# Row operations of the norms on VectorE instead of GpSimd, and two attention heads weighed side by side

## The chip, the cores and the metric

The kernel runs on one core of a Trainium2 chip. The metric is the device time of one execution in microseconds (us), as the median of several runs. A core has five engines that run in parallel and meet by semaphores: TensorE (PE in the profile, with its weight loads as PEld), VectorE (DVE), ScalarE (ACT), GpSimd (POOL) and SyncE (SP), whose queue here issues the DMAs.

## The reference, cut to what matters

Two layers work on 256 latent tokens (a grid of 4 rows of 64) and 256 context tokens, all of width 1024 in float32.

- Layer 0 mixes the tokens with 8 heads of neighbourhood attention (head width 64) beside 4 heads of a bidirectional recurrence (HGRN2), then a dense SwiGLU feed-forward layer (FFN).
- Layer 1 mixes with 4 heads of retention, then a top-2-of-8 SwiGLU mixture of experts.

```python
# neighbourhood attention: one softmax over the grid window and all context keys
p = softmax(concat([q @ k_band + bias, q @ k_ctx]))        # latent queries: 512 keys
o = p[band] @ v_band + p[ctx] @ v_ctx
a_c = full_attention(nc_q, nc_k, nc_v)                      # context queries: 256 keys
# after each of the four sub-layers (post-norm)
x = layer_norm(ALPHA * x + gate * y) * g + b
ctx = layer_norm(ALPHA * ctx + gate_c * y_c) * g + b        # layer 0 only
```

## The kernel before

All weights come from HBM by DMAs on SP's queue. Most float32 products are made of three matmuls on "fp32r" operands (`mm3`, lines 128 to 130): a value is split into a rounded high part (ScalarE copies it, `whi`) and a rest (VectorE subtracts, `wlo`). Such a matmul has one TensorE instruction; a plain float32 matmul has two. The order of instructions on each engine is set at build time by a list scheduler that may interleave stages; each engine then runs its list strictly in order.

The stages, with their times in the profile:

- **Layer 0 mixing (to about 362 us).** For each of 4 indices, `head_in` projects one HGRN head and runs its chain, and `pair(j)` projects and runs two attention heads (`na_pair`, line 569). For head `i` of a pair the tile `qs[:, i]` holds the high part of the queries in 64 partitions and their rest in the other 64, and `ks[:, i]` holds the high part of the keys in both halves. `score` (lines 581 to 584) makes one matmul over 128 partitions (high and rest of q times high of k) and one over 64 partitions (high of q times the rest of k, `kl`). Scores of 128 latent queries get their bias (L594), a softmax (`softmax`, L557 to L566), four transposes (L598), a copy to SBUF (L599), and are weighed with the values in `pm` (L603), one head after the other: each head writes 64 of the 128 output columns of the array, at `tile_position=(0, 64 * i)`. The context queries follow (L611 to L615). `ax_new` hands out the two PSUM banks of scores and transposes.
- **Output projection, norm, FFN (362 to 800 us).** `after0(i)` normalises row tile `i` of the residual stream `R` (tiles 0 and 1 latent, 2 and 3 context, 128 x 1024 each). `spread` transposes tiles into `h` for the next layer (ScalarE writes the high part, VectorE the rest, L236). The norm's scale and shift reach `h` by other coefficients, so that `R` itself needs `g` and `b` only at its next addition. That is `finish_ln`: two GpSimd operations for each row tile (L666, L667). For the latent tiles it is called right behind their `spread`, for the context tiles in `spread_ctx0`, and again in `after1` behind the FFN.
- **Retention (800 to about 1085 us)**, by heads `hd`, with weights through a ring of four buffers `raw` (`wload`).
- **Routing and experts (from about 1085 us).** `rows_in` (line 1118) writes the normalised rows in a high part and a rest (`xnl`, a GpSimd subtraction, L1125). `residual` (line 1060) scales and shifts `R` on GpSimd during the first expert.

```python
def finish_ln(i):
    nc.gpsimd.tensor_mul(R[i], R[i], lnrow[0])
    nc.gpsimd.tensor_add(R[i], R[i], lnrow[1])
```

Of the kernel before, what the change touches and what calls it, by code (L numbers as in the profile page):

```python
# [16 lines left out]
D = 1024  # L17
KD = 8
T = 512
# [69 lines left out]
def hybrid_kernel(ctx: ExitStack, tc: tile.TileContext, a, out):  # L89
# [479 lines left out]
    def na_pair(j, pq, pk, pt_new, pm):  # L569

        qs, ks = (phg.tile([128, 2, T], F32R, name=nm, tag=nm) for nm in ("qs", "ks"))
        kl = phg.tile([128, T], F32R, name="kl", tag="kk")
        for i in range(2):
            r, z = slice(64 * i, 64 * i + 64), slice(64 - 64 * i, 128 - 64 * i)
            nc.scalar.mul(qs[r, i, :], pq[r, :], 0.125)
            nc.vector.scalar_tensor_tensor(qs[z, i, :], pq[r, :], 0.125, qs[r, i, :], op0=OP.mult, op1=OP.subtract)
            nc.scalar.copy(ks[r, i, :], pk[r, :])
            nc.scalar.copy(ks[z, i, :], pk[r, :])
            nc.vector.tensor_sub(kl[r, :], pk[r, :], ks[r, i, :])

        def score(S, i, qc, kc):
            r = slice(64 * i, 64 * i + 64)
            nc.tensor.matmul(S, qs[:, i, qc], ks[:, i, kc], start=True, stop=False)
            nc.tensor.matmul(S, qs[r, i, qc], kl[r, kc], start=False, stop=True)

        for i in range(2):
            hh = 2 * j + i
            bias = arr("bias", [128, 2, 256])
            nc.sync.dma_start(bias, a["bias"][hh].rearrange("(t p) k -> p t k", p=128))
            pt2 = arr("pt2", [128, 4, 256])  # L590
            for t in range(2):
                S = ax_new()
                score(S, i, slice(t * 128, t * 128 + 128), slice(0, T))
                nc.vector.tensor_add(S[:, 0:256], S[:, 0:256], bias[:, t, :])  # L594
# [4 lines left out]
                nc.scalar.copy(pt2[:, :, t * 128:t * 128 + 128], pt.rearrange("p (c q) -> p c q", c=4))  # L599
            r = slice(64 * i, 64 * i + 64)  # L600
            vs = slice(hh * 64, hh * 64 + 64)
            for c in range(4):
                nc.tensor.matmul(pm[r, 0:256], nv[:, c, vs], pt2[:, c, :], start=(c == 0), stop=(c == 3), tile_position=(0, 64 * i))  # L603
            S = ax_new()
            for t in range(2):
                score(S[:, t * 256:t * 256 + 256], i, slice(256 + t * 128, 256 + t * 128 + 128), slice(256, T))
            E = softmax(S, 2, 256)
            pt = pt_new()
            for t in range(2):
                for c in range(2):  # L610
                    nc.tensor.transpose(pt[:, c * 256 + t * 128:c * 256 + t * 128 + 128], E[:, t * 256 + c * 128:t * 256 + c * 128 + 128], ident)  # L611
            ptc = phg.tile([128, 2, 256], F32, name="ptc", tag="f0")
            nc.scalar.copy(ptc, pt.rearrange("p (c q) -> p c q", c=2))
            for c in range(2):
                nc.tensor.matmul(pm[r, 256:512], nv[:, 2 + c, vs], ptc[:, c, :], start=(c == 0), stop=(c == 1), tile_position=(0, 64 * i))  # L615
        put_mix(j, pm)
# [47 lines left out]

    def finish_ln(i):
        nc.gpsimd.tensor_mul(R[i], R[i], lnrow[0])  # L666
        nc.gpsimd.tensor_add(R[i], R[i], lnrow[1])  # L667

# [6 lines left out]
    def after0(i):  # L675
        normalise(pb, R[i], "ln0")
        if i == 2:
            spread(0, "f0", h)
            finish_ln(0)
            finish_ln(1)  # L680

# [5 lines left out]
    def spread_ctx0():  # L687
        spread(1, "f0", h)
        finish_ln(2)
        finish_ln(3)  # L690

# [24 lines left out]
    for half, (t0, t1) in enumerate(((0, 6), (6, 11))):  # L716
# [3 lines left out]
        for f in range(nf):  # L720
# [11 lines left out]
            else:  # L732
                ada_next(0 if j < 8 else 1)
                for x, w in zip(p, wt):
                    mul_T(x, w, h, slice(0, 512))
            u = pb.tile([128, T], F32, name="u", tag="u", bufs=2)
            nc.scalar.activation(u, p[0], AF.Silu)
# [3 lines left out]
        if half:  # L741
# [12 lines left out]
            h = new_h("h1", KD, T)  # L754
            ln_rows(0, 1)

        def after1(i):
            normalise(pb, R[i], "ln1")
            if i == 2:
                spread(0, "a1", h)  # L760
                finish_ln(0)
                finish_ln(1)

# [8 lines left out]
    def spread_ctx1():  # L772
        spread(1, "a1", h)


# [58 lines left out]
    for hd in range(4):  # L834
# [56 lines left out]
        if hd:  # L891
            gates(hd)
        og = cnew("og", [128, 2, 512], 1)
        for t in range(2):
# [165 lines left out]
    def residual():  # L1060
# [551 lines left out]
```

## Time and profile before

| | |
|---|---|
| median of 3 runs | 2005.65 us (2003.67 to 2009.47) |
| the profiled execution | 2005.2 us, its span 2003.4 us |
| mean granted TensorE clock | 0.980 of full speed |
| busy, share of the span | PE 96%, PEld 69%, DVE 62%, ACT 41%, POOL 4% |
| DMA | 510 MB, mean 255 GB/s |

The span is the time from the first to the last instruction of the profiled execution; 1.8 us lie around it. A busy PE is not a PE at its peak: an instruction counts from its start to its modelled end, and successive matmuls overlap, so the pace of matmuls is read from one start to the next. "<-" behind an idle time names what ended it.

### The profile page before, as it was taken

How to read it: one execution, taken by the hardware profiler on the slowest of the kernel's cores; microseconds unless marked ns; L12 is line 12 of the kernel's file. 1: busy time of each engine (PE TensorE's matmuls, PEld its weight loads, DVE VectorE, ACT ScalarE, POOL GpSimd, SP SyncE). 2: the span in 40 equal slices, each digit the busy share in tenths (PEclk: the TensorE clock that was granted, in tenths of full speed). 3: DMA queues.
4: the chain of work that ended last, by engine and by line, in shares of the span. 5: the costliest groups of instructions: out<-in, count | busy, mean ns of one | idle time of the engine just before them, and what ended most of it. 6: DMA issues, size and time to landing. Idle time of an engine off the chain costs nothing. (4 is left out here: it accounts for less than half of the span.)

```text
span 2003.4 us, 24686 instructions
## 1 busy us (share of the span) xinstructions
PE 1926.9 (96%) x9143; PEld 1374.8 (69%) x9143; DVE 1241.9 (62%) x2020; ACT 830.8 (41%) x1080; POOL 78.6 (4%) x71
## 2 busy tenths in 40 slices
PE   8999999979999999899999999999999999999995
PEld 4887776658878878788888437853588338878731
DVE  4747775684587667865656518850588138888703
ACT  3435554233332332634433216730476026777500
POOL 0010000120000000100000210000000010000000
PEclk9999999989999999899999899999899999999998
DMA  7322233653356553323358899999999999999896
GB/s 296 137 92 88 91 98 107 215 199 128 124 167 208 185 185 116 127 85 116 111 201 310 324 414 396 375 345 420 418 416 367 388 420 420 413 341 375 316 410 241
DMA packets 94896, 510.00 MB, mean 255 GB/s; under 512 B 11312, under 2 KB 14000, under 8 KB 51760
## 3 DMA queue, kind: packets, MB, share of 16 engines
q1 hardware_dynamic: 94768, 508.34, 67.5%
q8 instruction: 74, 1.21, 0.3%
q14 instruction: 54, 0.44, 0.1%
HBM read 507.25 MB, written 1.05 MB: 254 GB/s over the span
## 5 line engine op out<-in xcount | busy, mean ns | idle before, releaser
L974 DVE TENSOR_TENSOR mlo<-mraw,mhi 128x2048 fp32r<-128x2048 f32 x168 | 378.3, 2286 | 37.5 <-ACT mhi L970 37.3
L202 ACT CAST whi<-raw 128x1024 fp32r<-128x1024 f32 x170 | 178.4, 1052 | 363.7 <-PE bank L129 216.0
L970 ACT CAST mhi<-mraw 128x2048 fp32r<-128x2048 f32 x168 | 312.3, 1910 | 24.0 <-PE bank L130 24.0
L203 DVE TENSOR_TENSOR wlo<-raw,whi 128x1024 fp32r<-128x1024 f32 x170 | 208.5, 1229 | 122.4 <-ACT whi L202 119.2
L130 PE MATMUL bank<-h0h,wlo 128*128 128x512 f32 (+1 forms) x656 | 250.7, 383 | 9.4 <-DVE wlo L203 9.4
L128 PE MATMUL bank<-h0h,whi 128*128 128x512 f32 (+1 forms) x656 | 252.1, 385 | 4.8 <-ACT whi L202 4.6
L129 PE MATMUL bank<-h0l,whi 128*128 128x512 f32 (+1 forms) x656 | 251.1, 383 | 4.5 <-DVE h0l L236 4.5
L1260 DVE TENSOR_TENSOR g<-g,bank 64x512 f32<-64x512 f32 x28 | 19.0, 679 | 236.6 <-ACT g L1259 236.6
L1256 PE MATMUL bank<-mraw,xg_145.75_15_12_8059 128*64 128x512 f32 x672 | 154.5, 601 | 0.8 <-DMA mraw<-in_moe_w 0.8
L130 PEld LDWEIGHTS bank<-h0h,wlo 128*128 128x128 f32 x656 | 126.5, 193 | 32.1 <-DVE wlo L203 10.2
L128 PEld LDWEIGHTS bank<-h0h,whi 128*128 128x128 f32 x656 | 125.6, 192 | 31.0 <-ACT whi L202 5.2
L129 PEld LDWEIGHTS bank<-h0l,whi 128*128 128x128 f32 x656 | 126.0, 192 | 28.2 <-DVE h0l L236 5.5
L128 PE MATMUL bank<-mhi,xg_145.75_15_14_8404 128*128 128x512 f32 x336 | 134.0, 400 | 4.9 <-ACT mhi L970 4.9
L129 PE MATMUL bank<-mlo,xg_145.75_15_14_8404 128*128 128x512 f32 x336 | 135.5, 403 | 2.5 <-DVE mlo L974 2.4
L128 PE MATMUL bank<-whi,h0h 128*128 128x512 f32 x288 | 114.7, 401 | 2.2 <-ACT whi L202 1.6
L130 PE MATMUL bank<-whi,h0l 128*128 128x512 f32 x288 | 113.9, 396 | 0.0
L129 PE MATMUL bank<-wlo,h0h 128*128 128x512 f32 x288 | 113.2, 395 | 0.0
L1256 PEld LDWEIGHTS bank<-mraw,xg_145.75_15_12_8059 128*64 128x64 f32 x672 | 47.4, 138 | 92.1 <-issue 88.7
L1259 ACT ACTIVATE g<-bank 64x512 f32<-64x512 f32 x28 | 16.6, 594 | 222.2 <-PE bank L1256 222.2
L130 PE MATMUL bank<-mhi,xg_145.75_15_15_8405 128*128 128x512 f32 x224 | 89.2, 398 | 0.0
L130 PE MATMUL bank<-mhi,xg_145.75_15_16_9605 128*128 128x512 f32 x224 | 88.6, 396 | 0.0
L129 PEld LDWEIGHTS bank<-mlo,xg_145.75_15_14_8404 128*128 128x128 f32 x336 | 64.8, 193 | 20.6 <-DVE mlo L974 5.9
(518 smaller groups left out, 3378.8 us busy)
## 6 DMA issues: line engine op xcount, KB each, us to landing
mraw<-in_moe_w SPq DMA_DIRECT2D x336, 1024.0 KB, 8.5
aw<-in_ada_u SPq DMA_DIRECT2D x96, 512.0 KB, 4.4
raw<-in_o_w_nat SPq DMA_DIRECT2D x32, 512.0 KB, 3.6
raw<-in_ffn_w1T SPq DMA_DIRECT2D x22, 512.0 KB, 4.6
raw<-in_ffn_w3T SPq DMA_DIRECT2D x22, 512.0 KB, 3.6
raw<-in_ffn_w SPq DMA_DIRECT2D x22, 512.0 KB, 3.7
raw<-in_e_w_T SPq DMA_DIRECT2D x20, 512.0 KB, 3.6
raw<-in_o_w_T SPq DMA_DIRECT2D x16, 512.0 KB, 3.6
```

What stands on the lines that cost most here:

```text
L128: nc.tensor.matmul(ps, l[0], r[0], start=first, stop=False)
L129: nc.tensor.matmul(ps, l[0], r[1], start=False, stop=False)
L130: return nc.tensor.matmul(ps, l[1], r[0], start=False, stop=last)
L202: nc.scalar.copy(hi, raw)
L203: nc.vector.tensor_sub(lo, raw, hi)
L970: x = nc.scalar.copy(hi, raw)
L974: y = eng.tensor_sub(lo[:, c], raw[:, c], hi[:, c])
L1256: nc.tensor.matmul(ps[64 * m:64 * m + 64, :], x[:, kk, :], w[:, k, :], start=(kk == 0), stop=(kk == KD - 1), tile_position=(0, 64 * m))
L1259: silu.append(nc.scalar.activation(g, ps[64:128, :], AF.Silu))
L1260: nc.vector.tensor_mul(g, g, ps[0:64, :])
```

## The change

- `finish_ln` becomes eight half-width operations for two row tiles on VectorE (four for each tile, 128 x 512 each). For the four tiles of layer 0's first norm it is called in the FFN's blocks 2 to 5, one tile in each. For the two latent tiles of the second norm it is called in the retention's head 1 (`rows_ready`), from two rows loaded into two of the four `raw` buffers; the load into `lnrow` is dropped. `residual` uses it too, and `rows_in` subtracts on VectorE.
- In `na_pair` the loop over query tiles goes outside, the loop over heads inside. `kl` is one tile for each head, its rest of k in both halves, so that the second matmul of `score` also takes 128 partitions (that adds the product of the two rests). The weighing of both heads is issued together, alternating between the two halves of the array's columns (`weigh`): for each 128 latent queries, and once for the 256 context queries. The bias is loaded for both heads and one query tile at a time, the same bytes.

```diff
     def finish_ln(i, rows):
-        nc.gpsimd.tensor_mul(R[i], R[i], lnrow[0])
-        nc.gpsimd.tensor_add(R[i], R[i], lnrow[1])
+        for c in (slice(0, 512), slice(512, D)):
+            nc.vector.tensor_mul(R[i][:, c], R[i][:, c], rows[0][:, c])
+            nc.vector.tensor_add(R[i][:, c], R[i][:, c], rows[1][:, c])
...
# after0, spread_ctx0, after1
-            finish_ln(...)
# FFN, block j
+                if 2 <= j < 6:
+                    finish_ln(j - 2, lnrow)
# before after1
-            ln_rows(0, 1)
+    def rows_ready():
+        rows = [wp.tile([128, D], F32, name="raw", tag="raw", bufs=4) for _ in range(2)]
+        for t, nm in zip(rows, ("ln_g", "ln_b")):
+            nc.sync.dma_start(t, a[nm][0, 1:2, :].to_broadcast([128, D]))
+        for i in range(2):
+            finish_ln(i, rows)
# retention, behind gates(hd)
+        if hd == 1:
+            rows_ready()
# residual
-            nc.gpsimd.tensor_mul(R[i], R[i], t[:, 0, :])
-            nc.gpsimd.tensor_add(R[i], R[i], t[:, 1, :])
+            finish_ln(i, (t[:, 0, :], t[:, 1, :]))
# rows_in
-            nc.gpsimd.tensor_sub(xnl[:, i, c], R[i][:, c], xnh[:, i, c])
+            nc.vector.tensor_sub(xnl[:, i, c], R[i][:, c], xnh[:, i, c])
# na_pair
-            nc.vector.tensor_sub(kl[r, :], pk[r, :], ks[r, i, :])
+            for x in (r, z):
+                nc.vector.tensor_sub(kl[i][x, :], pk[r, :], ks[r, i, :])
...
-            nc.tensor.matmul(S, qs[r, i, qc], kl[r, kc], start=False, stop=True)
+            nc.tensor.matmul(S, qs[:, i, qc], kl[i][:, kc], start=False, stop=True)
...
+        def weigh(c, first, last, cols, p):
+            for i in range(2):
+                vs = slice((2 * j + i) * 64, (2 * j + i) * 64 + 64)
+                nc.tensor.matmul(pm[64 * i:64 * i + 64, cols], nv[:, c, vs], p[i], start=first, stop=last, tile_position=(0, 64 * i))
+        for t in range(2):
+            q = slice(t * 128, t * 128 + 128)
+            nc.sync.dma_start(bias, a["bias"][2 * j:2 * j + 2, q].rearrange("h p k -> p h k"))
+            for i in range(2):
...                                  # score, bias, softmax, transposes, copy of head i
             for c in range(4):
-                nc.tensor.matmul(pm[r, 0:256], nv[:, c, vs], pt2[:, c, :], start=(c == 0), stop=(c == 3), tile_position=(0, 64 * i))
+                weigh(c, c == 0, c == 3, q, [pt2[:, i, c, :] for i in range(2)])
...                                  # both heads' context scores, then
+        for c in range(2):
+            weigh(2 + c, c == 0, c == 1, slice(256, 512), [x[:, c, :] for x in ptc])
```

The new tiles share addresses with tiles of the HGRN head: the second `kl` with its `f1`, the second `ptc` with its `q` (the first ones already shared with `kk` and `f0`).

## Rows read from the trace of the kernel before

**Rows 1.** Windows: length, busy PE, PEld, DVE, ACT, POOL; clock, DMA share, GB/s.
```profile
134.00:362.00 228.00, 227.19 (x1215) 162.90 (x1216) 157.70 (x410) 111.89 (x203) 0.00 (x0) 1.00 0.31 101
398.60:440.40 41.80, 28.18 (x196) 21.71 (x196) 34.30 (x63) 17.46 (x30) 15.29 (x7) 0.84 0.51 172
803.70:820.00 16.30, 9.43 (x53) 8.86 (x52) 14.06 (x30) 9.50 (x13) 4.38 (x2) 0.69 0.22 66
480.00:600.00 120.00, 120.00 (x538) 95.89 (x537) 77.12 (x148) 39.16 (x92) 0.00 (x0) 1.00 0.42 137
850.00:1040.00 190.00, 190.00 (x955) 161.09 (x954) 109.54 (x211) 80.33 (x108) 10.61 (x8) 1.00 0.37 117
1130.00:1200.00 70.00, 69.13 (x332) 25.22 (x328) 24.84 (x82) 12.32 (x29) 12.98 (x12) 1.00 1.01 413
```
**Rows 2.** Timeline of PE, a score of 512 keys: start, length, line, shapes.
```profile
177.98 0.39 PE L130 MATMUL bank<-h0h,wlo 128*128 128x512 f32 x1
178.21 0.39 PE L583 MATMUL bank<-ks,qs 128*128 128x512 f32 x1
178.52 0.50 PE L584 MATMUL bank<-kl,qs 64*128 64x512 f32 x1
178.95 0.38 PE L532 MATMUL bank<-hv,attc 128*128 128x128 f32 x1
```
**Rows 3.** Timeline of PE, scores of context queries, 256 keys.
```profile
181.23 0.38 PE L583 MATMUL bank<-ks,qs 128*128 128x256 f32 x1
181.55 0.38 PE L584 MATMUL bank<-kl,qs 64*128 64x256 f32 x1
181.86 0.38 PE L583 MATMUL bank<-ks,qs 128*128 128x256 f32 x1
```
**Rows 4.** Timeline of PE, the weighing of one head, latent then context queries.
```profile
184.26 1.94 PE L603 MATMUL bank<-pt,nv 128*64 128x256 f32 x8
186.13 0.66 PE L611 MATMUL bank<-ident,E 128*128 128x128 f32 x4
...
189.65 1.08 PE L615 MATMUL bank<-ptc,nv 128*64 128x256 f32 x4
```
**Rows 5.** Timeline of PE and PEld in the small expert: matmuls in both column halves.
```profile
1162.75 0.60 PE L1256 MATMUL bank<-mraw,xg_145.75_15_12_8059 128*64 128x512 f32 x2
1163.18 3.60 PE L1245 MATMUL bank<-mraw,_145.75_178.75_16_4_8147 128*64 128x512 f32 x16
...
1163.18 0.14 PEld L1245 LDWEIGHTS bank<-mraw,_145.75_178.75_16_4_8147 128*64 128x64 f32 x2 [0.28 <-issue]
```
**Rows 6.** Timeline of POOL and DVE behind the first norm.
```profile
394.14 4.95 POOL L666 TENSOR_TENSOR s_183.75_199.75_8_2_2622<-s_183.75_199.75_8_2_2622,nrow_183.75_9_0_2623 128x1024 f32<-128x1024 f32 x2 [286.25 <-ACT h0h L230]
...
396.82 2.56 DVE L236 TENSOR_TENSOR h0l<-tm_183.75_9_17_2995,h0h 128x256 fp32r<-128x256 f32 x1
...
404.51 0.42 DVE L236 TENSOR_TENSOR h0l<-tm_183.75_9_18_2999,h0h 128x256 fp32r<-128x256 f32 x1
```
**Rows 7.** Timeline of PE behind the first norm, its two longest waits.
```profile
407.18 0.58 PE L130 MATMUL bank<-h0h,wlo 128*128 128x256 f32 x1 [7.16 <-DVE wlo L203]
...
428.61 0.58 PE L129 MATMUL bank<-h0l,whi 128*128 128x256 f32 x1 [3.78 <-DVE h0l L236]
```
**Rows 8.** Timeline of DVE in the routing, one operation without and with GpSimd busy.
```profile
1102.68 0.23 DVE L1141 TENSOR_SCALAR oh_199.75_201_17_10_7825<-ids_199.75_201_17_1_7571,ix_199.75_201_17_16_7993 128x8 f32<-128x8 f32 x1
...
1106.29 1.18 DVE L1141 TENSOR_SCALAR oh_199.75_201_17_10_7825<-ids_199.75_201_17_1_7571,ix_199.75_201_17_16_7993 128x8 f32<-128x8 f32 x1
```
**Rows 9.** Timeline of DVE at the end: a half-width row operation.
```profile
1999.53 0.69 DVE L1519 TENSOR_TENSOR 45.75_178.75_16_15_15949<-45.75_178.75_16_15_15949,mraw 128x512 f32<-128x512 f32 x1
```
**Rows 10.** The tile kl: durations in ns, min/median/max, first and last start.
```profile
L579 DVE TENSOR_TENSOR kl<-bank,ks x8: 676/692/695, 172.7 to 323.9; 64x512 fp32r<-64x512 f32 x8
```
**Rows 11.** Waits of SP's queue, 130 to 400 us: total, times, longest.
```profile
SPq L589 <- DVE bank L594: 20.6, 4, 10.6
```
**Rows 12.** The page's DMA issues: count, size each, us from issue to landing.
```profile
raw<-in_o_w_nat SPq DMA_DIRECT2D x32, 512.0 KB, 3.6
```

More of the change, by code (lines that the diff above doesn't have):

```diff
@@ L571, in na_pair @@
         qs, ks = (phg.tile([128, 2, T], F32R, name=nm, tag=nm) for nm in ("qs", "ks"))
-        kl = phg.tile([128, T], F32R, name="kl", tag="kk")
+        kl = [phg.tile([128, T], F32R, name=f"kl{i}", tag=nm) for i, nm in enumerate(("kk", "f1"))]
         for i in range(2):
@@ L578, in na_pair @@
             nc.scalar.copy(ks[z, i, :], pk[r, :])
-            nc.vector.tensor_sub(kl[r, :], pk[r, :], ks[r, i, :])
+            for x in (r, z):
+                nc.vector.tensor_sub(kl[i][x, :], pk[r, :], ks[r, i, :])
         def score(S, i, qc, kc):
-            r = slice(64 * i, 64 * i + 64)
             nc.tensor.matmul(S, qs[:, i, qc], ks[:, i, kc], start=True, stop=False)
-            nc.tensor.matmul(S, qs[r, i, qc], kl[r, kc], start=False, stop=True)
-        for i in range(2):
-            hh = 2 * j + i
+            nc.tensor.matmul(S, qs[:, i, qc], kl[i][:, kc], start=False, stop=True)
[5 more added lines that the diff above has]
+            q = slice(t * 128, t * 128 + 128)
             bias = arr("bias", [128, 2, 256])
-            nc.sync.dma_start(bias, a["bias"][hh].rearrange("(t p) k -> p t k", p=128))
-            pt2 = arr("pt2", [128, 4, 256])
-            for t in range(2):
+            nc.sync.dma_start(bias, a["bias"][2 * j:2 * j + 2, q].rearrange("h p k -> p h k"))
+            pt2 = arr("pt2", [128, 2, 4, 128])
+            for i in range(2):
                 S = ax_new()
-                score(S, i, slice(t * 128, t * 128 + 128), slice(0, T))
-                nc.vector.tensor_add(S[:, 0:256], S[:, 0:256], bias[:, t, :])
+                score(S, i, q, slice(0, T))
+                nc.vector.tensor_add(S[:, 0:256], S[:, 0:256], bias[:, i, :])
                 E = softmax(S, 1, 512)
@@ L598, in na_pair @@
                     nc.tensor.transpose(pt[:, c * 128:c * 128 + 128], E[:, c * 128:c * 128 + 128], ident)
-                nc.scalar.copy(pt2[:, :, t * 128:t * 128 + 128], pt.rearrange("p (c q) -> p c q", c=4))
-            r = slice(64 * i, 64 * i + 64)
-            vs = slice(hh * 64, hh * 64 + 64)
+                nc.scalar.copy(pt2[:, i], pt.rearrange("p (c q) -> p c q", c=4))
             for c in range(4):
-                nc.tensor.matmul(pm[r, 0:256], nv[:, c, vs], pt2[:, c, :], start=(c == 0), stop=(c == 3), tile_position=(0, 64 * i))
+                weigh(c, c == 0, c == 3, q, [pt2[:, i, c, :] for i in range(2)])
+        ptc = [phg.tile([128, 2, 256], F32, name=f"ptc{i}", tag=nm) for i, nm in enumerate(("f0", "q"))]
+        for i in range(2):
             S = ax_new()
@@ L611, in na_pair @@
                     nc.tensor.transpose(pt[:, c * 256 + t * 128:c * 256 + t * 128 + 128], E[:, t * 256 + c * 128:t * 256 + c * 128 + 128], ident)
[L612 to L615, printed above, removed]
+            nc.scalar.copy(ptc[i], pt.rearrange("p (c q) -> p c q", c=2))
+        for c in range(2):
+            weigh(2 + c, c == 0, c == 1, slice(256, 512), [x[:, c, :] for x in ptc])
         put_mix(j, pm)
@@ L663, in ln_rows, with finish_ln @@
             nc.sync.dma_start(t, a[nm][l, i:i + 1, :].to_broadcast([128, D]))
-    def finish_ln(i):
-        nc.gpsimd.tensor_mul(R[i], R[i], lnrow[0])
-        nc.gpsimd.tensor_add(R[i], R[i], lnrow[1])
+    def finish_ln(i, rows):
+        for c in (slice(0, 512), slice(512, D)):
+            nc.vector.tensor_mul(R[i][:, c], R[i][:, c], rows[0][:, c])
+            nc.vector.tensor_add(R[i][:, c], R[i][:, c], rows[1][:, c])
     ln_rows(0, 0)
@@ L678, in after0 @@
             spread(0, "f0", h)
-            finish_ln(0)
-            finish_ln(1)
     for n in range(2):
@@ L688, in spread_ctx0 @@
         spread(1, "f0", h)
-        finish_ln(2)
-        finish_ln(3)
     gate[5] = [gate_row(pb, 0, 5, f"g5{s}", f"g{s}") for s in range(2)]
@@ L760, in after1 @@
                 spread(0, "a1", h)
-                finish_ln(0)
-                finish_ln(1)
         for n in range(2):
@@ L773, in spread_ctx1 @@
         spread(1, "a1", h)
+    def rows_ready():
+        rows = [wp.tile([128, D], F32, name="raw", tag="raw", bufs=4) for _ in range(2)]
+        for t, nm in zip(rows, ("ln_g", "ln_b")):
+            nc.sync.dma_start(t, a[nm][0, 1:2, :].to_broadcast([128, D]))
+        for i in range(2):
+            finish_ln(i, rows)
     o_in, o_inT, o_out = a["o_w_nat"], a["o_w_T"], a["o_w_out"]
```

## The prediction

> **What bounds the kernel now.** I read the windows first, stage by stage, then the timelines of the engines inside the stages that the change touches, then the waits. The windows show three kinds of stage [rows 1]. In the mixing of layer 0 (134 to 362 us), in the FFN (480 to 600) and in the retention (850 to 1040) TensorE is busy practically all the time, while VectorE has room: 157.7 of 228 us, 77 of 120, 110 of 190. There only TensorE's own work counts. Behind the two norms of layer 0 (398.6 to 440.4, 803.7 to 820) TensorE idles for 13.6 and 6.9 us, VectorE is busy for 34.3 of 41.8 and 14.1 of 16.3 us, GpSimd works at the same time, and the granted clock is 0.84 and 0.69 on the mean, so that part of TensorE's work there ran at the lower level of 1.2 GHz instead of 2.4, right behind its waits. In the experts (1130 to 1200 stands for them) the DMA engines are full. Their weights are loaded into buffers that earlier stages free, so that a microsecond saved before the experts should arrive at the end whole.
>
> **GpSimd stops VectorE.** The subtraction L236 takes 0.42 us alone, and 2.56 us while L666 runs on GpSimd [rows 6]. TensorE then waits 7.16 us for a rest of the weights and 3.78 us for a rest of `h`, both from VectorE [rows 7]. So the work on GpSimd is not beside the critical chain; it holds the engine that feeds it.
>
> **The attention pays for changing the shape of the array.** A matmul of 512 columns over 128 partitions follows its predecessor by 0.23 us (177.98 to 178.21). The second one of a score uses 64 partitions: it starts 0.31 us behind the first, and the next full one 0.43 us behind it [rows 2].
>
> **Part by part, TensorE in layer 0.**
> Scores of 512 keys: 0.31 + 0.43 = 0.74 us for two matmuls that take 0.23 each in a run of one shape, so 0.28 us too much. There are 16 (4 pairs, 2 heads, 2 query tiles): 4.5 us. Scores of 256 keys: 0.32 + 0.31 = 0.63 us [rows 3], where two halves of 0.23 are 0.23 together: 0.40 too much, 16 times, 6.4 us. With 128 partitions in both matmuls these 10.9 us go.
> Weighing: a head's eight instructions for the latent queries hold TensorE for 1.87 us, from 184.26 to 186.13, and the four for the context queries for about 1.01 (1.08 less the 0.07 by which the first group runs on past the next start) [rows 4]. With 0.09 for changing the shape on entry (0.32 against 0.23, as at the score) that is 1.96 and 1.10, eight times each: 24.5 us. In the small expert two matmuls of 64 output columns each start together, and the next two 0.43 us later (1162.75 to 1163.18), sixteen in about 8 x 0.43 [rows 5]. So the two halves of the array do run side by side, with 512 columns. A pair of 128 columns would then take a quarter of 0.43, 0.107 us. A query tile's sixteen instructions are eight such pairs, 0.86 us, and with a change of shape in and out (1.96 less 8 x 0.214, 0.25 us) 1.11; eight tiles make 8.9 us. The context's eight instructions of 256 columns are four pairs of 0.214 and 0.25, 1.11 us, four times 4.4 us. The sum is 13.3, and 11.2 us go.
> Together 22.1 us of TensorE. Against that VectorE gets eight more subtractions at 0.69 us [rows 10], 5.5 us, and would be busy 163 us of some 206, or 79%. That is under TensorE, but the softmax is a chain through three engines and two banks, and chains now hidden will show where the cover is thinner. I take three quarters, 16.5 us: nearer to the upper end of 22, because no wait of TensorE shows in this stage now. The lower end is 5.
>
> **The first norm's rests.** At best the window of 41.8 us shrinks to TensorE's work at full clock: 28.2 x 0.84 = 23.7 us, a gain of 18.1. VectorE would allow it: GpSimd's 15.3 us in the window are some six operations of 2.5 us (4.95 for two [rows 6]), and each holds one subtraction for 2.14 us, 12.8 us in all; 34.3 less 12.8 is 21.5 us. The context tiles' chain of statistics and the loads for the gates still stand in sequence, so I take 15; the lower end is 9, half.
>
> **The second norm's rests.** In 16.3 us TensorE works 9.43 at 0.69, 6.5 at full clock: 9.8 at most. VectorE's 14.1 us less GpSimd's 4.38 / 2.5 x 2.14 = 3.7 is 10.4, so 5.9 by VectorE. I take 5.5, with ends of 2 and 9.8.
>
> **Work that is moved.** Four operations of 0.69 us [rows 9] for a row tile are 2.8 us. Four tiles in the FFN add 11 us to VectorE, two in the retention 5.5; TensorE is busy throughout there and VectorE at 64 and 58% [rows 1], so I cost both at nothing. Without that cover it would be 16.5 us. The two new loads, 512 KB each by what they write, stand in SP's queue among the weights and hold two of four `raw` buffers for about 3.6 us of landing [rows 12] and 5.5 us of operations. DMA is busy for 0.37 there, and queued weights could be late by one landing: 0 to 4 us, I take 0. The load of `lnrow` that goes is one of the same size. `residual` puts 5.5 us on VectorE during the first expert, where the DMA is full and VectorE is busy for 25 of 70 us: nothing, and if the cover were gone, 5.5.
> In the routing four subtractions of 0.69 come onto VectorE's queue amid the chain that chooses the experts, at most 2.8 us. What goes there is GpSimd's hold: L1141 takes 1.18 instead of 0.23 us [rows 8]. I take 0, with 2 to either side.
> By the Trainium skill's page SBUF — State Buffer, section Who interferes with whom, GpSimd shuts out a VectorE instruction with two SBUF inputs. Rows 6 agree, 2.56 against 0.42. The page lets an instruction with one SBUF input pass, outside the wide modes. The tensor-scalar L1141, whose scalar also lies in SBUF, took 1.18 against 0.23 all the same. If only its table operand counted, that 0.95 us would have another cause and the routing would come out 1 us worse; I go by the rows.
>
> **The sum** is made against the profiled execution: 2005.2 - 16.5 - 15 - 5.5 = 1968.2 us, some 1968. Its 2005.2 lies 0.45 under the median of the runs, 2005.65, which is nothing at this size.
>
> **Rivals.**
> *The halves do not help at 128 columns* (0.12). The pair of loads in rows 5 lasts 0.14 us, longer than the 0.107 of a pair of matmuls with 128 columns. Were the loads not hidden, a pair would cost 0.25 us and a query tile 8 x 0.25 + 0.25 = 2.25; eight tiles 18.0 us against the 15.7 of now. The context groups would cost 4 x (0.214 + 0.14) + 0.25 = 1.67, four of them 6.7 against 8.8. The weighing would save nothing, the layer (10.9 + 0) x 0.75 = 8 us, and the time be 1977. For it: no row has so few columns in half an array. Against it: with 512 columns the loads are hidden whole. This is also the case in which part of the change does not do what it says.
> By the Trainium skill's page TensorE: Matmul & The Clock Gate, section The mechanism under row and column tiling, a weight load overlaps matmuls in flight when it goes to other rows of the array or to the background weight buffer; two column halves share their rows. Read strictly it speaks for this rival; rows 5, with no gap for the loads, speak against it.
> *The mixing is held by its chains* (0.14). The softmaxes of two heads now stand before one weighing, and the chain through VectorE and ScalarE is as long as before. Then only 5 us come, and the time is 1980. For it: VectorE at 79%. Against it: TensorE has no gap now.
> *The norms stay bound by something else* (0.12): the context tiles' statistics and ScalarE's casts follow each other whatever GpSimd does. Then half of 20.5 comes, and the time is 1978 or 1979. Both of these together (0.05): 1990.
> *Nearly all arrives* (0.08): 22 + 18 + 7, 1958.
> *Slower, by the bias loads* (0.04). There is one bias buffer; the second load of a pair now waits until both heads of the first query tile have been added, and SP's queue, with the weights behind it, waits along. Before, four such waits are 20.6 us, the longest 10.6 [rows 11], and TensorE never noticed. If each of the four second loads kept TensorE waiting by 10.6, that would be 42 us against the 37 gained: 2010. It decides from 9.3 us a pair.
> *No change* (0.02): gains and new waits cancel within 6 us.
> That leaves 0.43 for the forecast itself, 1960 to 1975.
>
> **How the numbers follow.** About 0.3%, 6 us, is what a measurement of this kernel can tell from no change. Only the last two cases lie within that or above; they have 0.06, and the chain cases could go a little further than priced, so faster has 0.93, same 0.03, slower 0.04. The range takes in the cases from 1958 to 1980 with the margin of the unknown terms (4 for the ring, 2 for the routing): 1955 to 1985. It leaves out 1990, no change, slower, and the ends where all lower or all upper bounds come together, under 0.2.
>
> **What would show it.** L583 and L584 at 0.23 us from start to start, and 0.12 with 256 columns; the sixteen instructions of L603's successor in about 1.1 us; no L236 above 0.5 us; TensorE's waits of 7.16 and 3.78 us gone, and the clock near 1.00 behind both norms; the FFN and the retention still without a gap on TensorE. It is wrong if TensorE shows new gaps between 134 and 362 us, if the window behind the first norm stays above 33 us, or if the retention waits for `raw`.

## The result, and the profile after

The changed kernel takes 1974.07 us (median of 4 runs, 1970.30 to 1976.10) against 2005.08 for the kernel before beside it. The ratio is 0.984, with a 95% interval of 0.9816 to 0.9863. The prediction was 1968.0, with a range of 1955 to 1985. The profiled execution took 1970.3 us, its span 1968.5; it is the fastest of the four.

First the windows that answer to [rows 1]; columns as there. The mixing is cut here from the first score to the last matmul of the output projection, once before and once after; the norms are cut where the same matmuls stand.

```profile
170.70:398.20 227.50, 225.82 (x1196) 159.88 (x1195) 154.56 (x401) 104.78 (x194) 4.06 (x2) 1.00 0.36 121
```
```profile
168.30:383.90 215.60, 211.62 (x1259) 156.37 (x1258) 160.33 (x421) 105.47 (x196) 0.00 (x0) 1.00 0.39 127
384.34:412.80 28.46, 24.81 (x196) 19.22 (x196) 25.26 (x59) 14.61 (x25) 0.00 (x0) 0.94 0.69 240
776.01:783.95 7.94, 7.32 (x56) 6.81 (x55) 7.79 (x19) 7.18 (x10) 0.00 (x0) 1.00 0.51 142
480.00:600.00 120.00, 120.00 (x539) 95.42 (x538) 85.72 (x172) 37.98 (x95) 0.00 (x0) 1.00 0.53 168
815.00:1005.00 190.00, 189.47 (x947) 160.09 (x947) 112.81 (x218) 80.27 (x108) 10.61 (x8) 1.00 0.38 122
```

The mixing lost 11.9 us; TensorE's busy time fell by 14.2 and its idle time rose from 1.7 to 4.0. The stretch behind the first norm fell from 41.8 to 28.5 us with the same 196 matmuls, that behind the second from 16.3 to 7.9. In the FFN TensorE is still busy throughout, and in the retention but for 0.5 us; VectorE is at 71% and 59% there.

The first norm's row operations are not among VectorE's work in the FFN, though the program calls them there. The list scheduler put them ahead, into the stretch behind the norm: they run between 378.6 and 417.2 us, none between 480 and 600 (the line's groups over the whole span: min/median/max in ns, first and last start; the other two groups, `cres` of L673 and `s` of L674, lie from 393.8 to 414.8):

```profile
L673 DVE TENSOR_TENSOR s_183.75_199.75_8_2_2664<-s_183.75_199.75_8_2_2664,nrow_183.75_9_0_2665 x4: 684/684/687, 378.6 to 398.4; 128x512 f32<-128x512 f32 x4
L674 DVE TENSOR_TENSOR cres_183.75_9_2_2667<-cres_183.75_9_2_2667,nrow_183.75_9_1_2666 x4: 680/684/686, 407.4 to 416.5; 128x512 f32<-128x512 f32 x4
```

Some twelve of the sixteen lie in the window of 28.46 us above, 8.2 of VectorE's 25.3 us. Behind the first norm the change therefore moved the work to another engine, but not out of the stretch. The second norm's operations ran late, from 872.0 to 882.4 us, since the load of their rows comes late.

The timeline of TensorE in the mixing, which answers to [rows 2 to 4]:

```profile
182.57 0.39 PE L129 MATMUL bank<-h0l,whi 128*128 128x512 f32 x1
182.89 0.43 PE L591 MATMUL bank<-pt,nv 128*64 128x128 f32 x2
183.25 0.50 PE L130 MATMUL bank<-h0h,wlo 128*128 128x512 f32 x1
...
185.21 0.39 PE L584 MATMUL bank<-ks,qs 128*128 128x512 f32 x1
185.43 0.39 PE L585 MATMUL bank<-kl,qs 128*128 128x512 f32 x1
185.66 0.38 PE L547 MATMUL bank<-ident,sgt 128*128 128x128 f32 x2
...
187.95 1.09 PE L591 MATMUL bank<-pt,nv 128*64 128x128 f32 x14
188.97 0.50 PE L584 MATMUL bank<-ks,qs 128*128 128x512 f32 x1
...
192.96 0.28 PE L584 MATMUL bank<-ks,qs 128*128 128x256 f32 x1
193.08 0.28 PE L585 MATMUL bank<-kl,qs 128*128 128x256 f32 x1
193.20 0.28 PE L584 MATMUL bank<-ks,qs 128*128 128x256 f32 x1
```

The scores run at 0.22 and, with 256 columns, 0.12 us from start to start, as forecast. The weighing doesn't come in one piece of sixteen instructions: two go out at 182.89 and fourteen at 187.95, with matmuls of the projections between. The two take 0.36 us, the fourteen 1.02.

VectorE behind the first norm, the answer to [rows 6] (the line's groups over the whole span: min/median/max in ns), and TensorE's waits behind the norm, the answer to [rows 7]:

```profile
L236 DVE TENSOR_TENSOR h0l<-tm_183.75_9_15_3024,h0h x8: 406/418/422, 380.8 to 798.6; 128x256 fp32r<-128x256 f32 x8
L236 DVE TENSOR_TENSOR h0l<-tm_183.75_9_18_3041,h0h x8: 418/425/427, 382.6 to 803.1; 128x256 fp32r<-128x256 f32 x8
```
```profile
386.18 0.66 PE L225 MATMUL bank<-ident,cres_183.75_9_2_2667 128*128 128x128 f32 x4 [0.40 <-DVE cres_183.75_9_2_2667 L177]
394.94 1.13 PE L271 MATMUL bank<-av,selb 128*128 128x256 f32 x4 [0.49 <-ACT av L261]
398.33 0.55 PE L225 MATMUL bank<-ident,cres_183.75_9_2_2667 128*128 128x128 f32 x3 [2.26 <-ACT cres_183.75_9_2_2667 L176]
```

No L236 takes over 0.43 us, and the waits of 7.16 and 3.78 us are gone. The longest that is left, 2.26 us, is for the context tiles' own normalisation on ScalarE.

**Where the time went.** The table cuts TensorE's timeline and SP's queue at the same instructions in each profiled execution (us). *Start*: to the first score. *Mixing*: to the last matmul of the output projection. *Norm 1*: to the first matmul of the FFN's second product. *Norm 2*: from the FFN's last matmul to the retention's first score. *Retention*: to the issue of the first expert load (`mraw`). *Experts*: from there to the end of the span. The FFN between the norms has 241.5 to 241.7 us in all of them.

| kernel | start | mixing | norm 1 | norm 2 | retention | experts |
|---|---|---|---|---|---|---|
| before | 170.75 | 227.44 | 163.34 | 44.14 | 161.4 | 994.7 |
| after | 168.29 | 215.64 | 150.00 | 35.78 | 162.2 | 995.0 |
| after, again | 171.76 | 216.01 | 151.47 | 35.63 | 162.5 | 995.6 |
| norms alone | 169.42 | 227.79 | 150.09 | 35.54 | 162.1 | 993.9 |
| pair alone | 167.91 | 215.67 | 161.83 | 45.13 | 161.4 | 994.6 |
| heads reversed | 168.15 | 209.07 | 151.93 | 35.84 | 162.1 | 996.3 |
| heads reversed, again | 169.52 | 208.60 | 152.29 | 35.85 | 162.4 | 995.9 |
| heads in turn | 169.82 | 219.93 | 149.68 | 36.05 | 162.5 | 994.2 |
| score of 64 partitions | 169.71 | 221.11 | 150.95 | 35.89 | 162.4 | 996.2 |
| VectorE, old places | 170.15 | 216.06 | 152.71 | 43.09 | 161.4 | 995.8 |
| GpSimd, new places | 170.81 | 215.83 | 161.57 | 35.48 | 161.3 | 996.2 |
| GpSimd, held back | 170.51 | 215.61 | 148.33 | 35.84 | 161.4 | 996.2 |
| reversed and held back | 171.18 | 210.30 | 149.96 | 35.58 | 161.3 | 993.7 |

From before to after: mixing -11.8, norm 1 -13.3, norm 2 -8.4, retention +0.8, experts +0.3, and -2.5 in the start, which the change doesn't touch (see the last section).

### The profile page after: what moved, and what is told of

Same layout as the page of the kernel before. It is cut to its first block, busy times and chain, and to the rows that moved or that the text cites. A ratio compares the mean times of both kernels' runs of the same rounds, so it can differ in the third digit from the quotient of the medians.

```text
span 1968.5 us, 24832 instructions
## 1 busy us (share of the span) xinstructions
PE 1904.2 (97%) x9207; PEld 1365.0 (69%) x9207; DVE 1233.9 (63%) x2064; ACT 830.7 (42%) x1080; POOL 34.2 (2%) x51
## 3 DMA queue, kind: packets, MB, share of 16 engines
HBM read 507.25 MB, written 1.05 MB: 258 GB/s over the span
## 5 line engine op out<-in xcount | busy, mean ns | idle before, releaser
L129 PEld LDWEIGHTS bank<-h0l,whi 128*128 128x128 f32 x656 | 123.7, 189 | 22.1 <-issue 1.3
```

What stands on the lines that cost most here:

```text
L129: nc.tensor.matmul(ps, l[0], r[1], start=False, stop=False)
```

## The experiments

**Each part alone, and the change again.** The first kernel takes the norms' and rests' part with the attention of before, the second the attention with the norms of before.

```diff
# norms alone, na_pair as before:
-            nc.tensor.matmul(S, qs[:, i, qc], kl[i][:, kc], start=False, stop=True)
+            nc.tensor.matmul(S, qs[r, i, qc], kl[r, kc], start=False, stop=True)
...
# pair alone, norms as before:
-        for c in (slice(0, 512), slice(512, D)):
-            nc.vector.tensor_mul(R[i][:, c], R[i][:, c], rows[0][:, c])
+        nc.gpsimd.tensor_mul(R[i], R[i], lnrow[0])
...
```

> The attention pair is that of the kernel before; the row operations are those of the changed kernel. Theory (GpSimd held VectorE behind the two norms): the profiled execution gains about 20.6 us, 13 behind the first norm and 8 behind the second, so some 1985, and no gap of TensorE above 3 us behind the norms. Rival (the norms gain only because the faster attention shifted the order of instructions): less than 10 us, above 1995.

> The attention pair is that of the changed kernel; all row operations stay on GpSimd as before. Theory (scores of one array shape save about 9 us, the weighing about 5): 14 us less than before, some 1991, and the last matmul of the output projection ends 14 us earlier. Rival (the pair saves nothing by itself): within 6 us of before.

> The changed kernel once more, beside the others on one chip: 1970 to 1976, the width of its first runs.

Measured: norms alone 1984.94 us, ratio 0.9898 (0.9883 to 0.9913); pair alone 1994.55, 0.9945 (0.9929 to 0.996); the change again 1974.97, 0.9842 (0.9829 to 0.9856), with 2005.91 for before on that chip. So 21.0 and 11.4 us add up to 32.4, where both together gave 30.9: the parts are independent within what the runs can tell, and the table shows it stage by stage. The norms alone came out as expected, without a wait of TensorE over 3 us behind them. The pair alone was expected at some 1991 and gained 3.5 us less, 11.4; its mixing fell by 11.8 where 14 were expected.

**The order of the heads in the weighing.** The split of the weighing above suggests that the scheduler sends the first head's product out as soon as its copy is there. The second head's copy comes last, so a list that begins with it can't begin early.

```diff
         def weigh(c, first, last, cols, p):
-            for i in range(2):
+            for i in (1, 0):
```

> The changed kernel with the second head first in each pair of weighing matmuls. In the changed kernel the first head's first product is issued alone as soon as its copy is there, so that each of 12 groups pays a second change of the array's shape and loses its partner: about 0.47 us for a query tile, 0.67 for the context. Theory: whole groups, 8 x 0.47 + 4 x 0.67 = 6.4 us less of TensorE, 4 to 7 us of time, so about 1966 to 1970 where the changed kernel has 1972. Rival (the splits fall into time that TensorE would have waited anyway): no difference beyond 2 us, or a loss because the first product now waits for the later head.

Measured: 1967.16 us, ratio 0.981 (0.9796 to 0.9823), 7.8 us less than the change again beside it and within the first figure. The timeline of TensorE in this kernel:

```profile
187.35 1.09 PE L591 MATMUL bank<-pt,nv 128*64 128x128 f32 x16
188.37 0.50 PE L584 MATMUL bank<-ks,qs 128*128 128x512 f32 x1
```

All sixteen take 1.02 us. Counted from each start to the next start, the weighing's lines hold TensorE for 23.0 us before, 17.6 after and 12.3 here; the scores' for 22.2, 13.0 and 13.7. So the split cost 5.3 us of matmul time, and the mixing fell by 6.6.

**Heads in turn.** Are the halves only side by side when neighbours in the list go to different halves?

```diff
-            for c in range(4):
-                weigh(c, c == 0, c == 3, q, [pt2[:, i, c, :] for i in range(2)])
+            for i in (1, 0):
+                for c in range(4):
+                    weigh(c, c == 0, c == 3, q, [pt2[:, x, c, :] for x in range(2)], i)
...
```

> Head 1 is weighed whole, then head 0, in place of product by product; everything else is as in the run with the heads' order reversed (1967.2 us). If two products run side by side because neighbours in the list go to different column halves of the array, each of the eight groups for 128 latent queries costs about 1.87 us in place of 1.0, and each of the four for the context queries as much: 12 x 0.86 = 10.3 us more, about 1977.5. Rival: the array holds two streams whatever the order, or a product of 128 columns is held by something other than its columns. Then nothing changes: 1966 to 1969.

Measured: 1975.54 us, ratio 0.9854 (0.9837 to 0.987). The median is near the first figure, for a reason that is only half the one given. The timeline of TensorE:

```profile
248.11 1.58 PE L591 MATMUL bank<-pt,nv 128*64 128x128 f32 x16
249.62 0.50 PE L584 MATMUL bank<-ks,qs 128*128 128x512 f32 x1
...
203.56 1.09 PE L591 MATMUL bank<-ptc,nv 128*64 128x256 f32 x8 [0.18 <-ACT ptc L620]
204.58 0.44 PE L265 MATMUL bank<-ident,av 128*128 128x128 f32 x2
...
263.12 1.06 PE L258 MATMUL bank<-aw,sT 128*32 128x256 f32 x2 [4.58 <-ACT E L562]
...
266.17 1.98 PE L591 MATMUL bank<-ptc,nv 128*64 128x256 f32 x8
268.08 0.67 PE L258 MATMUL bank<-aw,sT 128*32 128x256 f32 x6
```

Eight instructions of one half and then eight of the other take 1.51 us, not the expected 1.87: part of the second eight still runs beside the first. The trace starts the second half's first instruction 0.49 us behind the first half's first, together with its fifth. With four and four (the context queries) the second half starts at once, and three groups of four take 1.02, as when they alternate. In both cases the second half begins beside the fourth from last instruction of the first. So neighbours needn't alternate strictly; the second half's work must only come soon. The fourth group takes 1.91 for another reason, the clock. Its window, columns as above, shows a granted clock of 0.50, the lower level:

```profile
266.17:268.08 1.91, 1.91 (x12) 0.79 (x8) 0.00 (x0) 0.00 (x0) 0.00 (x0) 0.50 0.31 109
```

The clock fell towards the end of TensorE's wait of 4.58 us (0.92 on the mean from 258 to 262 us, 0.50 from 262 to 263) and was back at full speed by 269.

The lines of the weighing together make 4.8 us of the stage's 10.9, of which 0.9 is the clock in that group. Of the rest some 2.4 is other busy time, part of it in the same slow stretch, and 3.7 idle time (8.4 against 4.7 us). Of that, 2.8 are waits of L258 for a bank that a softmax (L562) still reads, 5.1 us in place of 2.3, so the new order of the list has a price of its own.

**The score's second matmul with 64 partitions.** This separates the scores' gain from the weighing's.

```diff
-            for x in (r, z):
-                nc.vector.tensor_sub(kl[i][x, :], pk[r, :], ks[r, i, :])
+            nc.vector.tensor_sub(kl[i][r, :], pk[r, :], ks[r, i, :])
...
-            nc.tensor.matmul(S, qs[:, i, qc], kl[i][:, kc], start=False, stop=True)
+            r = slice(64 * i, 64 * i + 64)
+            nc.tensor.matmul(S, qs[r, i, qc], kl[i][r, kc], start=False, stop=True)
```

> As the changed kernel, but the second matmul of each score takes 64 partitions again, and the second copy of the keys' rest isn't made. TensorE's time in the scores fell by 9.3 us from before to after (22.25 to 12.96 from start to next start). If that is the gain of this part, it comes back whole, since TensorE has no gap there: 1982 to 1985. Rival, the softmax chains hide it and the gain in this stage is the weighing's: 1974 to 1977.

Measured: 1978.27 us (median of three runs), ratio 0.986 (0.984 to 0.988), between the two. Its window of the mixing, to be set beside the one of after:

```profile
169.70:390.80 221.10, 219.89 (x1259) 159.23 (x1258) 156.16 (x413) 106.00 (x197) 0.00 (x0) 1.00 0.37 124
```

The scores hold TensorE for 22.2 us again, 9.2 more than after; the stage is 5.5 us longer. With the slower scores TensorE idles for 1.2 us, with the faster ones for 4.0. So 2.8 us of the scores' gain went into waits. The softmax chain (`ptc`, `E`) accounts for 1.3 of it and a gate's row from VectorE for 0.8; these were covered until then.

**The norms: which engine, and when.** First VectorE at the old places, right behind each norm.

```diff
# after0, spread_ctx0, after1: called again right behind each spread
+            finish_ln(...)
# before after1, as in the kernel before
+            ln_rows(0, 1)
# FFN and retention
-                if 2 <= j < 6:
-                    finish_ln(j - 2, lnrow)
-            rows_ready()
```

> As the changed kernel, but the norms' scale and shift are called at the old places, right behind each norm, on VectorE. If the time counts more than the engine: VectorE feeds TensorE there, and four tiles at 2.8 us put up to 11 us into the window behind the first norm and 5.5 into that behind the second; most of it shows, 1984 to 1990. Rival, only GpSimd's hold was the trouble: VectorE fits the operations into its free time, 1974 to 1978.

Measured: 2125.14 us, ratio 1.0605 (1.0588 to 1.0623). The edit stood one loop too far out and scaled the second norm's tiles four times over, so nothing behind that norm can be read, and neither figure is tested; norm 1 took 153.7 us. The same with each tile scaled once:

> As the changed kernel, but the norms' scale and shift are called at the old places, right behind each norm, on VectorE, each once. The run before this one multiplied the two latent tiles of the second norm four times over; of it only the first norm can be read, where the way from the last product of the output projection to the FFN's second half took 153.7 us, against 150.0 in the changed kernel and 163.3 before. So at the first norm the engine gives 9.6 us and the time 3.7. If the second norm divides alike, it loses 2 to 5.5 us, and the whole comes to 1980 to 1983. Rival, the time of the call is nothing by itself: 1974 to 1977.

Measured: 1983.09 us, ratio 0.9888 (0.9869 to 0.9907), at the upper end of the first figure. The two norms don't divide alike. Norm 1 took 152.7 us (153.7 in the run above), 9.7 to 10.6 under before and 0.4 to 4 over the kernels with VectorE at the new places. Those few us are not the price of the time, as the expectation has it: here the row operations run from 380.8 to 417.6 us, in the changed kernel from 378.6 to 417.2. What differs is their order within the stretch. Norm 2 took 43.1, only 1.05 under before; there the times do differ, 780.6 us on against 872.0. Its timeline of VectorE and then of TensorE shows why:

```profile
782.66 1.28 DVE L674 TENSOR_TENSOR s_183.75_199.75_8_2_2664<-s_183.75_199.75_8_2_2664,nrow_183.75_9_1_2666 128x512 f32<-128x512 f32 x2
783.87 1.28 DVE L673 TENSOR_TENSOR s_183.75_199.75_8_2_2664<-s_183.75_199.75_8_2_2664,nrow_183.75_9_0_2665 128x512 f32<-128x512 f32 x2
785.07 1.29 DVE L674 TENSOR_TENSOR s_183.75_199.75_8_2_2664<-s_183.75_199.75_8_2_2664,nrow_183.75_9_1_2666 128x512 f32<-128x512 f32 x2
786.27 0.68 DVE L661 TENSOR_TENSOR gt_183.75_9_6_2864<-bank,g_183.75_9_4_2670 128x512 f32<-128x512 f32 x1
```
```profile
787.01 0.33 PE L225 MATMUL bank<-ident,cres_183.75_9_2_2667 128*128 128x128 f32 x1 [3.07 <-DVE gt_183.75_9_6_2864 L661]
```

Row operations that nobody needs yet stand ahead of the one that TensorE waits for. So at the second norm it is the time that counts.

Then GpSimd at the new places (`residual` stays on VectorE):

```diff
-    def finish_ln(i, rows):
+    def finish_ln(i, rows, eng=nc.gpsimd):
...
-            nc.vector.tensor_mul(R[i][:, c], R[i][:, c], rows[0][:, c])
-            nc.vector.tensor_add(R[i][:, c], R[i][:, c], rows[1][:, c])
+            eng.tensor_mul(R[i][:, c], R[i][:, c], rows[0][:, c])
+            eng.tensor_add(R[i][:, c], R[i][:, c], rows[1][:, c])
```

> As the changed kernel, but the norms' scale and shift stay on GpSimd, at the new places (FFN blocks 2 to 5, retention head 1), in half-width operations. If the time counts more than the engine: VectorE is stopped for some 4 to 5 us in each FFN block of about 30 us in which it has a third of its time free, TensorE keeps its pace, 1973 to 1978. Rival, a stopped VectorE is felt wherever it is, since it prepares every weight: six tiles at 4.3 us, up to 26 us of new waits in the FFN and the retention, 1985 to 2000.

Measured: 1984.21 us, ratio 0.9894 (0.9877 to 0.991). The timeline of GpSimd:

```profile
381.33 2.82 POOL L673 TENSOR_TENSOR s_183.75_199.75_8_2_2664<-s_183.75_199.75_8_2_2664,nrow_183.75_9_0_2665 128x512 f32<-128x512 f32 x2 [273.38 <-PE bank L225]
...
885.82 6.82 POOL L673 TENSOR_TENSOR s_183.75_199.75_8_2_2664<-s_183.75_199.75_8_2_2664,raw 128x512 f32<-128x512 f32 x4 [5.33 <-DMA raw<-in_ln_g]
```

The first norm's operations weren't late: GpSimd has nothing ahead of them in its list, so it began at 381 us, as soon as the inputs were there. The second norm's waited for the loads of the scale rows and ran at 886 us. Norm 2 accordingly takes 35.5 us, as in the changed kernel, and norm 1 161.6, nearly as before. The time lies between the two figures of the expectation, because the premise of both, late operations, holds for one norm only. At the first norm the run parts the engines instead: VectorE, with the operations at the same times, takes 149.7 to 153.7 us, so there GpSimd costs some 8 to 12 us by being GpSimd. To make the first norm's operations late on GpSimd, their inputs must come late. `held` and `zero` are tiles of 128x1, `zero` holds zeros, and `u` is from the FFN block before:

```diff
                 if 2 <= j < 6:
+                    nc.gpsimd.tensor_mul(held, u[:, 0:1], zero)
+                    nc.gpsimd.tensor_add(lnrow[0][:, 0:1], lnrow[0][:, 0:1], held)
+                    nc.gpsimd.tensor_add(lnrow[0][:, 512:513], lnrow[0][:, 512:513], held)
                     finish_ln(j - 2, lnrow)
```

> In the run before this one, GpSimd had nothing ahead in its list and began the first norm's operations as soon as their inputs were there, at 381 to 393 and 409 to 421 us, whatever their place in the program; so it was not late. Here a tiny product of the FFN block before is added (as zero) to the scale row first, so that GpSimd can't begin a tile before that block is done. If a stopped VectorE is hidden in the FFN, whose TensorE is busy throughout while VectorE has a third of its time free, the first norm is as fast as in the changed kernel: 1973 to 1977. Rival, it is felt there too: four tiles at 4.3 us, 1980 to 1992.

Measured: 1971.86 us, ratio 0.9833 (0.9816 to 0.9849), as fast as the changed kernel or a little faster, and 1.1 us under the lower end of the first figure. Its window in the FFN:

```profile
430.00:560.00 130.00, 130.00 (x580) 104.76 (x579) 79.42 (x138) 42.02 (x88) 26.11 (x23) 1.00 0.44 142
```

GpSimd works for 26.1 us there, and TensorE has no gap. So the operations can be taken out of the way in two ways. At the first norm another engine is enough: GpSimd in the stretch costs 11.6 to 13.3 us against GpSimd held back (161.6 against 148.3 and, in the last pair below, 150.0), VectorE in the stretch 1.5 or so (150.0 and 151.5 in the changed kernel). At the second norm the time decides: late, either engine takes 35.5 to 36.1 us; early, VectorE costs 7.3 us more (43.1 against 35.8) and GpSimd 8.4 to 9.3 (44.1 and 45.1).

**The best of both.** The reversed order together with the held-back GpSimd, and beside it the reversed order again.

> The order of heads reversed in the weighing, together with the norms' scale and shift on GpSimd, held back into the FFN and the retention. Alone the first took 1967.2 us (6.9 under the changed kernel), the second 1971.9 (2.2 under it, within what the runs tell apart). If both are real and independent: 1964 to 1966. Rival, the second was chance: 1966 to 1969, as the reversed order alone.

> The kernel with the order of heads reversed once more, on the same chip as the one beside it, to compare the two and to see how far its median repeats: 1966 to 1970.

Measured: 1964.90 us, ratio 0.9794 (0.978 to 0.9808), and 1964.14, 0.979 (0.9776 to 0.9804): the same. The reversed order alone came out below its expected 1966 to 1970, so the 1964.90 shows no further gain from holding GpSimd back. The better version of the change is the one with one line reversed, some 2% under before.

## Why the prediction was right, and where its terms were off

**Weighing, predicted 11.2 us, measured 5.5** (23.0 to 17.6). The failed step is "A query tile's sixteen instructions are eight such pairs". They are in the program's text, but the scheduler parted each of the twelve groups. Each split leaves a product without a partner and pays one more change of shape. The price of whole groups was about right: 1.02 us measured for the sixteen, 1.11 forecast, and 10.8 us gained in the kernel with the heads reversed.

**Scores, predicted 10.9, measured 9.3.** The paces were right, 0.22 and 0.12. What is missing is that not all of them keep that pace: of the 32 matmuls with 512 columns 14 hold TensorE for 0.28 us or more. Some follow another shape, as at 188.97, and pay the change as before; others follow their own shape (238.35, 295.83, 324.30), and what holds those isn't shown.

**Three quarters of that, 16.5, measured 11.8.** Of the 14.8 us that the two lines lost, 11.8 arrived, four fifths. The discount was of about the right size, for a reason that is half right: TensorE's idle time rose from 1.7 to 4.0 us, and of these 2.3 us 1.3 are waits for the softmax chain, most of it the line of `ptc`. The rest is a weight load (`aw`) and other small waits. Two of TensorE's waits in the mixing after:

```profile
PE bank L591 <- ACT ptc L619: 1.0, 2, 0.9
PE bank L258 <- DMA aw<-in_ada_u: 1.1, 2, 0.9
```

So the sign of being wrong "if TensorE shows new gaps between 134 and 362 us" did come, though small. It was the 22.1 in front of the discount that was too large. In the kernel with the heads reversed 18.4 of 19.3 us arrived, so the share isn't a constant; it depends on the scheduler's order too.

**First norm, predicted 15, measured 13.3** (11.9 in the second execution). The window is 28.5 us, under the 33 that was named as the bound; the clock is 0.94, not near 1.00: it is at 0.50 from 399.5 to 402.4, right behind the wait of 2.26 us for the context tiles' normalisation, which is left, as the step "the context tiles' chain of statistics" said. **Second norm, predicted 5.5, measured 8.4.** The bound by VectorE, 5.9, supposed that 10.4 us of its work remain in the stretch, and it does 7.8 there. It counted GpSimd's hold only within the window, 4.38 us, but the hold began 5.5 us before it, and VectorE came into the stretch late. These are GpSimd's rows before:

```profile
798.16 4.94 POOL L666 TENSOR_TENSOR s_183.75_199.75_8_2_2622<-s_183.75_199.75_8_2_2622,nrow_183.75_9_0_2623 128x1024 f32<-128x1024 f32 x2 [367.39 <-PE bank L225]
803.06 5.02 POOL L667 TENSOR_TENSOR s_183.75_199.75_8_2_2622<-s_183.75_199.75_8_2_2622,nrow_183.75_9_1_2624 128x1024 f32<-128x1024 f32 x2
```

That term was sized too small. TensorE's idle time fell from 6.9 to 0.6 us and the clock rose from 0.69 to 1.00. The bound by TensorE, 9.8, was the one that held. The step "GpSimd stops VectorE" stands for the first norm, where the engine alone made the gain. At the second the experiments add what the prediction hadn't parted: VectorE, called at GpSimd's old places, saves only 1.05 of the 8.4 us.

**Moved work, predicted 0.** The FFN has the same time to 0.2 us, but not because TensorE covers the operations: none ran there, so for VectorE that step isn't tested. That the FFN can cover such work is shown with GpSimd held back. In the retention VectorE's operations cost 0.8 us (162.2 against 161.4), of it 0.5 a wait of TensorE for `v` from VectorE; with GpSimd there instead and the same loads it is 161.3 to 161.4, so the `raw` ring costs nothing. **Routing, predicted 0 within 2.** The operation of [rows 8] takes its short time each time:

```profile
1066.54 0.23 DVE L1152 TENSOR_SCALAR oh_199.75_201_17_9_7878<-ids_199.75_201_17_1_7625,ix_199.75_201_17_14_8040 128x8 f32<-128x8 f32 x1
1067.68 0.22 DVE L1152 TENSOR_SCALAR oh_199.75_201_17_10_7879<-ids_199.75_201_17_1_7625,ix_199.75_201_17_16_8047 128x8 f32<-128x8 f32 x1
```

From the logits to the small expert it is 15.9 us against 16.8, so 0.95 came, as much as one such hold, and with the pair alone, whose subtraction stays on GpSimd, it is 16.8 again. By the Trainium skill's page SBUF — State Buffer, section Who interferes with whom, a VectorE instruction with one SBUF input passes beside GpSimd outside the wide modes. Here 1.18 became 0.22 to 0.23 us with GpSimd gone, so the hold was GpSimd's, as the prediction took it from its rows. Whether the operation ran in a wide mode no run shows, so this doesn't speak against the page. Whether anything of it reached the end can't be told: the experts' time, counted from their first load at 973.5 us, differs by 2.6 us between kernels.

**A microsecond saved before the experts arrives whole.** Right to within 2.6 us, with the first expert load as the mark: from there to the end all kernels take 993.7 to 996.3 us.

**The rivals.** That the halves don't help at 128 columns is refuted by sixteen instructions in 1.02 us, where that case had 2.25. By the Trainium skill's page TensorE: Matmul & The Clock Gate, section The mechanism under row and column tiling, a weight load is pulled ahead of matmuls in flight when it goes to other rows of the array or to the background weight buffer. Here both halves use the same rows, and their loads, 0.13 to 0.14 us each, some 2.2 for sixteen one after another, lie under the 1.02; the rule for other rows alone doesn't cover that, and no run shows whether the buffer does. That the mixing is held by its chains is true for some 1.3 us of waits, not for 11. The norms were not bound by something else. The bias loads (issued by L596) wait on SP's queue for 6.1 and 13.2 us in the two largest groups, while TensorE's waits in the mixing are for other things, the largest 1.1 us in all for `aw`:

```profile
SPq L596 <- DVE ss L537: 13.2, 3, 11.0
...
SPq L596 <- DVE bank L601: 6.1, 3, 2.8
```

**The sum.** 37 us forecast; without the start the stages give 11.8 + 13.3 + 8.4 - 0.8 - 0.3 = 32.4, and the medians 31.0. The mixing came out 4.7 us smaller than forecast and the first norm 1.7, the retention and the experts cost 1.1, and the second norm gave 2.9 more. So the errors partly cancel, and that the profiled execution comes within 2.3 us of 1968 is partly luck: 2.5 us of its gain lie in the start, which the change doesn't touch. The median is 6 us above.

## What to carry to other kernels

Work that nobody waits for yet must not stand in the way of the engine that feeds TensorE. On another engine it can hold that one (the first norm, 11.6 us); on the same engine it can stand ahead of what is needed (the second norm, 7.3 us); behind it, it cost under 1 us on either. Look in the trace for the time at which an operation ran: a place in the program moves nothing where a scheduler, or an engine with an empty list, takes the operation as soon as its inputs are there; in these runs only a late input did. Where a gain depends on instructions standing next to each other, look in the order that was issued, not in the source, and begin the group with the operand that comes last.

## What was not expected of the hardware

The same matmuls of the start run at two paces in different executions. Here are rows of TensorE's timeline, first before, then after:

```profile
18.16 0.63 PE L129 MATMUL bank<-wlo,h0h 128*128 128x512 f32 x1
18.59 0.63 PE L130 MATMUL bank<-whi,h0l 128*128 128x512 f32 x1
19.02 0.63 PE L128 MATMUL bank<-whi,h0h 128*128 128x512 f32 x1
```
```profile
17.06 0.39 PE L129 MATMUL bank<-wlo,h0h 128*128 128x512 f32 x1
17.29 0.39 PE L130 MATMUL bank<-whi,h0l 128*128 128x512 f32 x1
17.52 0.40 PE L128 MATMUL bank<-whi,h0h 128*128 128x512 f32 x1
```

From start to start it is 0.43 us in the one and 0.23 in the other. In the kernel before the pace changes from 0.43 to 0.23 at 21.2 us, and from then on it is the same in both:

```profile
23.34 0.39 PE L130 MATMUL bank<-whi,h0l 128*128 128x512 f32 x1
23.57 0.40 PE L129 MATMUL bank<-wlo,h0h 128*128 128x512 f32 x1
```

This looks like the clock. The trace's records of the granted clock begin at 21.2 us before and at 13.3 us after, in both at full speed; ahead of the first record a window has nothing to go by and prints 1.00. And 0.43 for 512 columns is the pace of the lower level: behind the second norm before, from 812 to 816 us, 256 columns follow each other by 0.21 where a clock of 0.50 is on record. The table's start column follows the time of that first record, from 12.7 us with the pair alone (167.9) to 22.3 in the changed kernel again (171.8); over the executions only two whose records lie 0.1 us apart stand the other way round. So the -2.5 us of the start go with the clock and not with the change, and between the two executions of the changed kernel it is 3.5 of the 6.1 us by which their spans differ. What sets the time at which the clock first rises stays open.

The second surprise is the overlap of the column halves without strict alternation, 1.51 us for eight and eight where 1.87 was expected.
